# A hybrid attention and Fourier encoder on one core: stores at the end of the step, a second z buffer, one v load per block, and a new order of the side work

## The chip, the core and the metric

The kernel runs on one core of a Trainium2 chip. The core has five engines that run side by side and meet only through semaphores: TensorE (PE, matmuls; its weight loads are listed as PEld), VectorE (DVE), ScalarE (ACT), GpSimd (POOL) and SyncE (SP), which here issues nearly all transfers between the device memory and the core's own memory (SBUF). Every engine takes its instructions in the order in which the program has them; an instruction that waits holds all behind it on its engine. Matmul results lie in PSUM, which VectorE and ScalarE can read and GpSimd can't. The metric is the device time of one execution in microseconds.

## The reference

One encoder layer is applied to two sequences, a prompt of 256 tokens and a sample of 2048, each of width 1024. Cut to what matters:

```python
h = rms_norm(x, g_pre)
q, k, v, z_a, u_f, z_f = split(h @ w_in, 6)         # six times 512 columns
y_a = neighbourhood_attention(q, k, v, rpb)         # 8 heads of 64; tokens on a grid 64 wide;
                                                    # softmax over a window of 8 rows x 16 columns, with bias
y_f = real(fft2(u_f groups)) @ w_fourier + b_fourier
mixed = concat(rms_norm(y_a, g_na) * silu(z_a), rms_norm(y_f, g_f) * silu(z_f))
out = x + rms_norm(mixed @ w_out, g_post)
```

All is in float32; the kernel splits each factor of a product into a high and a low part and makes three matmuls of it.

## The kernel before

The first 600 us project x into q, k, v, z and u, store them in device memory, and do the Fourier half up to its result y_f, also stored. What the change touches is the stage behind it, the attention steps, which run from about 600 to 855 us; after that comes an output stage of 18 token tiles, which adds the attention half's share of `mixed @ w_out` to the Fourier half's share (stored as `oD`) and writes the output.

**The steps.** There are 36 groups of queries: four pairs of heads, nine groups each (one of the prompt, eight of the sample: four row ranges R, two column halves hc). The main loop has one step k per group. In step k TensorE computes the scores of group k (`scores`, L1229), transposes the softmax weights of group k-1 (`transp`, L1573, in two halves) and multiplies them with v (`pv`, L1589). VectorE adds the bias and takes the maximum (`bias_max`, L1251), ScalarE takes exponentials (`exps`, L1256), VectorE the reciprocal of the sum (L1260), GpSimd scales the weights (L1263); the transposes are copied out of PSUM by ScalarE and VectorE (L1575, L1577, tile `pt`); at the end of a step VectorE multiplies the product with the gate za into y (L1603). The halves of `transp` share PSUM banks `ptb`, so the second waits for the first's copies.

**The loads.** At a step's end `prep_v` loads v and za of group k+1, and `prep` the q of group k+4. v has three buffers. A group's v comes in two column blocks; each block is cut into chunks of up to 128 tokens, and where the last chunk is short it is loaded by a transfer of its own (L1197 and L1199).

**The stores.** The Fourier share's output rows (`oD`, L1530 and L1735) are issued when the tile is ready, and y (`yD`, L1612) when a tile of it is: in every second step, right behind L1603. As SyncE goes in order, what comes behind a store waits until its data are there.

**The side work.** TensorE's order is written out by hand: between the attention's matmuls it runs the Fourier share of the output product, plainly (`f_mm`) up to step 15. From step 16 on two token tiles at a time are done by a scheme that needs 7 products of blocks in place of 8, over four steps (`p_mm`; a pair of tiles begins at steps 16, 20, 24, 28 and 32). Its sums, high and low parts and evacuations on the other engines are placed by a table, `AT`: each entry names an operation, the step relative to the pair's first, one of ten slots in the step (called by `side`), and an engine. The names that matter here, with n for the step relative to the pair's first:

- M0, M1: y_f times z of the pair's two tiles (GpSimd, L1702). z has one buffer in `sm`: the second tile's z is loaded (L1473) only once M0 has read the first's.
- HD, LD: high and low part of the first tile; A1 to A4: sums of the tiles (L1712); H21, L21: high part (a cast, L1716) and low part (L1720) of a sum; H3, L3, H4, L4: further parts.
- X0 to X3, Z0, Z1, Z1b, Z2: evacuations of the products px and pz from PSUM into output rows `ofs` (L1729 adds, L1731 and L1733 only scale).

A second table, `TS`, places the preparation of the combined weights (`t_load`, `t_scale`, `t_sum`, `t_hi`, `t_lo`) in steps 9 to 16. The scores, px and pz share PSUM banks: four score tiles a step, three of the tag that pz has too.

Of the kernel before, what the change touches and what calls it, by code (L numbers as in the profile page):

```python
# [10 lines left out]
F32 = mybir.dt.float32  # L11
# [6 lines left out]
TP, TS = 256, 2048  # L18
# [12 lines left out]
K0 = (0, 4, 12, 20)  # L31
# [143 lines left out]
def build(tc, A, O):  # L175
    nc = tc.nc
# [8 lines left out]
    vD = [dr.tile([32, w, 512], F32, name="vD%d" % i) for i, w in enumerate(KW)]  # L185
# [585 lines left out]
    for b in range(16):  # L771
# [29 lines left out]
        if kind % 2:  # L801
            i, d = p, o
# [380 lines left out]
    def prep_v(g):  # L1183
        cs = slice(g["pr"] * 128, g["pr"] * 128 + 128)
        g["v"] = jl.tile([128, 7, 128], F32, tag="v", name="v", bufs=VB)
        g["ch"], j = [], 0
        for b, (c0, w) in enumerate(g["t"]):
            n = g["nr"] * w
            if g["R"] is None:
                src = vP[b]  # L1190
            else:
                src = vD[2 * g["hc"] + b][K0[g["R"]]:K0[g["R"]] + g["nr"]]
            src = src.rearrange("r c e -> (r c) e")
            m = -(-n // 128)
            z = min(-(-n // m) + 7 & ~7, 128)
            f = n // z
            nc.sync.dma_start(g["v"][:z, j:j + f], src[:z * f, cs].rearrange("(j p) e -> p j e", p=z))  # L1197
            if n % z:
                nc.sync.dma_start(g["v"][:n % z, j + f], src[z * f:, cs])  # L1199
            ch = [(z * x, min(z, n - z * x), j + x) for x in range(m)]  # L1200
            g["ch"].append(ch)
            j += len(ch)
        g["za"] = jl.tile([128, 256], F32, tag="za", name="za", bufs=VB)
        nc.sync.dma_start(g["za"], zD[1, cs, g["ts"]])
# [246 lines left out]
        later.append(second)  # L1451

    later = []

    def run_later():
        while later:
# [10 lines left out]
        if half and z:  # L1467
            z_load(d)

    def z_load(d):  # L1470
        ts = slice(d["t"] * 128, d["t"] * 128 + 128)
        d["z"] = sm.tile([128, 4, 128], F32, tag="yz", name="yz", bufs=1)
        nc.sync.dma_start(d["z"], zD[0, :, ts].rearrange("(c p) t -> p c t", p=128))  # L1473

    def ys_mul(d):
# [57 lines left out]

# [48 lines left out]
    def pv(g):  # L1582
# [26 lines left out]
            nc.scalar.activation(s4, p4, AF.Square)  # L1609
            nc.gpsimd.tensor_tensor(out=view(ysq[:, ts]), in0=view(ysq[:, ts]), in1=s4, op=ALU.add)  # L1610
        if R is None or hc:
            nc.sync.dma_start(yD[0, pr, :, ts], y)  # L1612

    WO = [[None, None] for c in range(4)]

# [41 lines left out]
    def t_lo(j, x, e):  # L1657
# [4 lines left out]
        else:  # L1662
# [4 lines left out]
    TS = ((9, 2, t_load, 0), (9, 6, t_load, 1), (10, 4, t_scale, 0), (11, 3, t_sum, 0, 0, V),  # L1667
          (11, 7, t_sum, 0, 1, V), (11, 8, t_scale, 1), (11, 8, t_sum, 0, 2, nc.gpsimd), (12, 2, t_sum, 1, 0, V),
          (12, 5, t_sum, 0, 3, V), (12, 7, t_sum, 1, 1, nc.gpsimd), (12, 5, t_hi, 0, 0, qt), (12, 6, t_hi, 0, 1, gt),
          (13, 1, t_lo, 0, 0, V), (13, 4, t_sum, 1, 2, V), (13, 6, t_hi, 1, 0, gt), (13, 8, t_sum, 1, 3, V),  # L1670
          (14, 2, t_lo, 1, 0, V), (14, 5, t_lo, 0, 1, V), (14, 7, t_hi, 1, 1, qt), (16, 6, t_lo, 1, 1, V))

    def B_(name):
        n, x = {"11": (0, 0), "21": (0, 2), "22": (1, 2)}.get(name, (None, None))
# [25 lines left out]
    def o_mul(P, e, x):  # L1700
        d = P["d"][x]
        e.tensor_tensor(out=d["raw"], in0=d["raw"], in1=d["z"], op=ALU.mult)  # L1702
        if x == 0:
            z_load(P["d"][1])

    def o_sum(P, e, x):
        if x == 0:
# [14 lines left out]
    def o_out(P, e, p, x, n, first, last):  # L1722
# [9 lines left out]
        else:  # L1732
            nc.scalar.activation(o[:, ns], i, AF.Copy, scale=s)  # L1733
        if last:
            nc.sync.dma_start(oD[t * 128:t * 128 + 128, :], o)  # L1735
# [9 lines left out]
    AT = (("A3", -1, 8, nc.gpsimd), ("H21", 0, 2, V), ("X2", 2, 3, V), ("M0", -3, 7, nc.gpsimd), ("L4", 2, 0, V),  # L1745
          ("X3", 3, 5, V), ("Z1", 1, 7, V), ("L3", 1, 2, V), ("A1", -1, 0, nc.gpsimd), ("X0", 0, 4, nc.scalar),
          ("A2", -1, 7, nc.gpsimd), ("M1", -2, 8, nc.gpsimd), ("Z0", 0, 8, V), ("X1", 1, 5, nc.scalar),
          ("L21", 0, 4, V), ("Z1b", 1, 7, V), ("H3", 0, 6, nc.scalar), ("HD", -2, 6, nc.scalar),
          ("H4", 1, 8, nc.scalar), ("LD", -2, 7, V), ("A4", 0, 7, nc.gpsimd), ("Z2", 2, 7, V))

    def side(k, slot):
        pr, i = divmod(k, 9)
# [60 lines left out]
    for k in range(2, len(G) + 1):  # L1813
# [222 lines left out]
```

## Time and profile before

| | |
|---|---|
| three runs, median (lowest to highest) | 966.48 us (963.81 to 970.37) |
| the profiled execution | 968.52 us |
| its span, first to last instruction | 966.7 us |
| mean granted clock of TensorE | 0.998 |
| busy TensorE, VectorE, ScalarE, GpSimd | 948.1, 738.4, 503.3, 453.9 us |
| transfers | 271.90 MB, mean 281 GB/s |

In the rows of the profile a line ends with the idle time of the engine before it and what released it (`[1.47 <-DMA v<-vD]`). A group of waits is "who waited, for whom: us in total, times, longest". `out<-in` are the program's names: `pt<-ptb` is the copy of the transposes. SPq stands for SyncE's queue; its rows are the moments of issue, and a long one is an issue that was held. Matmuls overlap: each is drawn longer than the distance to the next. Step k begins with its first matmul of L1229: step 16 at 708.82 us, step 22 at 753.06, step 24 at 769.30.

### The profile page before, as it was taken

What the parts mean: (1) busy time and instruction counts of PE and PEld (TensorE: products, weight loads), DVE (VectorE), ACT (ScalarE), POOL (GpSimd) and SP (SyncE); (2) the same over time, 40 slices, a digit from 0 to 9 for tenths busy, and PEclk for the clock granted to TensorE, in tenths of its full rate; (3) what the DMA queues carried; (4) which work ended last, traced back from release to release, by engine and by line L of the source; (5) the groups of instructions that cost most, each with busy time, mean ns of one, the idle gap of its engine ahead of it and who ended that gap; (6) DMA issues with size and microseconds to landing.
All of it is one profiled execution on the core that took longest, in us unless ns stands there. A gap on an engine that the chain in (4) does not pass through costs nothing. (4 is left out here: it accounts for less than half of the span.)

```text
span 966.7 us, 16758 instructions
## 1 busy us (share of the span) xinstructions
PE 948.1 (98%) x5595; PEld 785.2 (81%) x5595; DVE 738.4 (76%) x1347; ACT 503.3 (52%) x1083; POOL 453.9 (47%) x431
## 2 busy tenths in 40 slices
PE   9999999999999999999999999999998999999996
PEld 8889988888888888888888789787777777888875
DVE  6758987878976755797877378776987788759777
ACT  6736675433225432333344277777865666744443
POOL 4100003364842102755654065666897798625444
PEclk9999999999999999999999999999999999999999
DMA  9799697566749882599889987779875999989996
GB/s 358 290 379 339 242 355 252 196 213 258 302 153 381 299 340 101 211 366 339 304 300 341 365 278 269 230 221 303 261 239 179 286 280 278 295 300 330 290 309 217
DMA packets 140654, 271.90 MB, mean 281 GB/s; under 512 B 13242, under 2 KB 80528, under 8 KB 137304
## 3 DMA queue, kind: packets, MB, share of 16 engines
q1 hardware_dynamic: 140216, 270.41, 80.8%
q8 instruction: 45, 0.74, 0.3%
q10 hardware_dynamic: 288, 0.40, 0.1%
q14 instruction: 41, 0.34, 0.1%
q0 software_dynamic: 64, 0.02, 0.0%
HBM read 181.10 MB, written 96.81 MB: 287 GB/s over the span
## 5 line engine op out<-in xcount | busy, mean ns | idle before, releaser
L164 PE MATMUL mm<-xh,wa 128*128 128x512 f32 x448 | 174.6, 390 | 0.0
L166 PE MATMUL mm<-xh,wa 128*128 128x512 f32 x448 | 174.5, 389 | 0.0
L165 PE MATMUL mm<-xl,wa 128*128 128x512 f32 x448 | 174.5, 389 | 0.0
L545 POOL TENSOR_TENSOR ws<-wr 128x512 f32<-128x512 f32 x16 | 22.5, 1405 | 220.7 <-PE mm L166 125.4
L1263 POOL TENSOR_SCALAR w<-w,m 128x465 f32<-128x465 f32 (+9 forms) x136 | 91.0, 681 | 30.6 <-DVE m L1260 20.6
L164 PEld LDWEIGHTS mm<-xh,wa 128*128 128x128 f32 x448 | 84.1, 188 | 17.5
L165 PEld LDWEIGHTS mm<-xl,wa 128*128 128x128 f32 x448 | 84.1, 188 | 17.5
L166 PEld LDWEIGHTS mm<-xh,wa 128*128 128x128 f32 x448 | 84.1, 188 | 17.4
L1500 PE MATMUL po<-wk,yh 128*128 128x512 f32 x280 | 87.2, 393 | 0.3 <-ACT yh L1486 0.3
L560 DVE TENSOR_TENSOR wa<-wr,wa 128x512 fp32r<-128x512 f32 x60 | 70.7, 1186 | 20.3 <-ACT wa L559 20.0
L1256 ACT ACTIVATE w<-w,m 128x465 f32<-128x465 f32 (+9 forms) x136 | 78.4, 579 | 13.7 <-DVE m L1251 13.3
L1963 POOL TENSOR_TENSOR xt<-of,xt 128x512 f32<-128x512 f32 x34 | 43.2, 1291 | 54.5 <-issue 32.9
L1251 DVE CUSTOM_DVE_ANT_1 w<-s,tb 128x465 f32<-128x465 f32 (+8 forms) x124 | 61.3, 529 | 8.9 <-PE s L1229 7.4
L598 POOL TENSOR_TENSOR mt<-mt,rmask 128x880 f32<-128x880 f32 (+2 forms) x24 | 51.2, 2146 | 32.1 <-DVE mt L594 25.8
L165 PE MATMUL mm<-vl,xh 128*128 128x512 f32 x168 | 65.4, 390 | 0.0
L164 PE MATMUL mm<-vh,xh 128*128 128x512 f32 x168 | 65.4, 389 | 0.0
L166 PE MATMUL mm<-vh,xl 128*128 128x512 f32 x168 | 65.4, 389 | 0.0
L1589 PE MATMUL pv<-pt,v 120*64 120x128 f32 (+9 forms) x880 | 58.4, 278 | 5.5 <-DMA v<-vD 3.7
L1589 PEld LDWEIGHTS pv<-pt,v 120*64 120x64 f32 (+9 forms) x880 | 48.3, 136 | 19.1 <-issue 9.2
L891 DVE TENSOR_TENSOR f<-u,mm 128x512 f32<-128x512 f32 x64 | 43.5, 679 | 26.5 <-PE mm L166 20.1
L1573 PE MATMUL ptb<-ident,w 128*120 128x128 f32 (+8 forms) x422 | 59.8, 277 | 1.9 <-DVE pt L1577 1.1
L1500 PEld LDWEIGHTS po<-wk,yh 128*128 128x128 f32 x280 | 52.0, 188 | 11.7 <-ACT yh L1486 1.0
(333 smaller groups left out, 2457.7 us busy)
## 6 DMA issues: line engine op xcount, KB each, us to landing
wr<-wz SPq DMA_DIRECT2D x48, 512.0 KB
vl<-sD SPq DMA_DIRECT2D x20, 512.0 KB
xm<-xm SPq DMA_DIRECT2D x9, 1024.0 KB
oD<-ofs SPq DMA_DIRECT2D x18, 512.0 KB
of<-oD SPq DMA_DIRECT2D x18, 512.0 KB
xt<-xn SPq DMA_DIRECT2D x18, 512.0 KB
yo<-xt SPq DMA_DIRECT2D x35, 256.0 KB
yr<-yD SPq DMA_DIRECT2D x34, 256.0 KB
```

The lines of the kernel that those rows point to most:

```text
L164: nc.tensor.matmul(out, lh, rh, start=first, stop=False)
L165: nc.tensor.matmul(out, lh, rl, start=False, stop=False)
L166: nc.tensor.matmul(out, ll, rh, start=False, stop=last)
L560: nc.vector.tensor_tensor(out=o[:, 1], in0=src, in1=o[:, 0].bitcast(F32), op=ALU.subtract)
L598: nc.gpsimd.tensor_tensor(out=o, in0=i, in1=rmask[:, m0:m0 + n].unsqueeze(2).to_broadcast([128, n, 80]), op=ALU.add)
L891: nc.vector.tensor_tensor(out=dst(f, b), in0=src(uu[u]), in1=src(p), op=op)
L1251: nc.vector.tensor_tensor_reduce(out=rows(g["w"][b][:, h, :n], w), in0=rows(g["s"][2 * b + h][:, :nr * sw(w)], sw(w))[:, :, :w], in1=tv, s ...
L1256: nc.scalar.activation(w, w, AF.Exp, bias=m[:, h:h + 1], scale=-1.0, accum_out=m[:, 2 + h:3 + h])
L1263: nc.gpsimd.tensor_scalar(w, w, m[:, 4 + h:5 + h], 1.0, ALU.mult, ALU.mult)
L1500: nc.tensor.matmul(p, (d["l"] if x == 2 else d["h"])[:, c], w(n, int(x == 1), c), start=j == 0, stop=j == 11)
L1573: nc.tensor.transpose(ptb[h][:nk, j * 128:j * 128 + 128], g["w"][b][:, h, c0:c0 + nk], ident)
L1589: nc.tensor.matmul(p[hs, b], g["v"][:nk, v, hs], g["pt"][b][:nk, h, j * 128:j * 128 + 128], start=j == 0, stop=j == len(ch) - 1)
```

## The change

Four things change.

- Stores of y and of the output rows go onto a list (`put`) and are issued at the end of the step (`put_all`), behind the loads of v, za and q.
- The second tile's z of a pair gets a buffer of its own (pool `gz`) and is loaded three steps ahead together with its y, no longer after M0.
- Where the source has enough rows, a block of v is loaded in one transfer; the last chunk then brings some rows that are not used.
- The tables `TS` and `AT` have new places: among others A2 goes from GpSimd to VectorE (step n = -1, slot 5), X3 from VectorE to ScalarE, H21 moves from slot 2 to slot 1, LD from slot 7 to 6, X2 from slot 3 to 6, M1 and A1 to slot 1 of n = -1, A3 to slot 3 of n = 0.

```diff
@@ prep_v
-            if g["R"] is None:
-                src = vP[b]
-            else:
-                src = vD[2 * g["hc"] + b][K0[g["R"]]:K0[g["R"]] + g["nr"]]
-            src = src.rearrange("r c e -> (r c) e")
+            src = (vP[b] if g["R"] is None else vD[2 * g["hc"] + b][K0[g["R"]]:]).rearrange("r c e -> (r c) e")
             m = -(-n // 128)
             z = min(-(-n // m) + 7 & ~7, 128)
-            f = n // z
+            f = m if src.shape[0] >= m * z else n // z
             nc.sync.dma_start(g["v"][:z, j:j + f], src[:z * f, cs].rearrange("(j p) e -> p j e", p=z))
-            if n % z:
-                nc.sync.dma_start(g["v"][:n % z, j + f], src[z * f:, cs])
+            if f < m:
+                nc.sync.dma_start(g["v"][:n - z * f, j + f], src[z * f:n, cs])
...
+    puts = []
+
+    def put(dst, src):
+        puts.append((dst, src))
+
+    def put_all():
+        while puts:
+            nc.sync.dma_start(*puts.pop(0))
...
-    def z_load(d):
+    def z_load(d, pool=None):
         ts = slice(d["t"] * 128, d["t"] * 128 + 128)
-        d["z"] = sm.tile([128, 4, 128], F32, tag="yz", name="yz", bufs=1)
+        d["z"] = (pool or sm).tile([128, 4, 128], F32, tag="yz", name="yz", bufs=1)
...
@@ f_evac, o_out
-            nc.sync.dma_start(oD[t * 128:t * 128 + 128, :], o)
+            put(oD[t * 128:t * 128 + 128, :], o)
@@ pv
-            nc.sync.dma_start(yD[0, pr, :, ts], y)
+            put(yD[0, pr, :, ts], y)
...
@@ o_mul
-        if x == 0:
-            z_load(P["d"][1])
@@ AT, two of its lines
-          ("A2", -1, 7, nc.gpsimd), ("M1", -2, 8, nc.gpsimd), ("Z0", 0, 8, V), ("X1", 1, 5, nc.scalar),
+          ("HD", -2, 5, nc.scalar), ("M0", -3, 9, nc.gpsimd), ("A2", -1, 5, V), ("X3", 3, 7, nc.scalar),
...
@@ side
                 ys_load(P["d"][1], False)
+                z_load(P["d"][1], gz)
@@ main loop, end of step k
             gq = pt.enter_context(tc.tile_pool(name="gq", bufs=7, side="right"))
+            gz = pt.enter_context(tc.tile_pool(name="gz", bufs=1, side="right"))
         if k + 1 < len(G):
             prep_v(G[k + 1])
         if k + 4 < len(G):
             prep(G[k + 4])
+        put_all()
```

What stands on the engines is shown at three places. The first is SyncE between the ends of steps 17 and 18, from za and q of one group to the next v: vP holds the prompt's v, vD0 and vD1 the sample's, tb is the bias table, oD and yD are the stores. Before:

```order
L1197 DMA v_7415<-vP_68 80x2x128 x2
L1204 DMA za_7418<-zD_69 128x256
L1180 DMA ql_7421<-qD_62 128x2x128
L1154 DMA tb_7423<-tD15_81 128x2400
L1735 DMA oD_77<-ofs_7262 128x1024
L1612 DMA yD_78<-y_7410 128x512
L1197 DMA v_7519<-vD0_64 128x128
L1199 DMA v_7519<-vD0_64 125x128
L1197 DMA v_7519<-vD1_65 120x2x128
L1199 DMA v_7519<-vD1_65 101x128
L1204 DMA za_7524<-zD_69 128x256
```

And now:

```order
L1193 DMA v_7400<-vP_68 80x2x128 x2
L1200 DMA za_7403<-zD_69 128x256
L1180 DMA ql_7406<-qD_62 128x2x128
L1154 DMA tb_7408<-tD15_81 128x2400
L1193 DMA v_7501<-vD0_64 128x2x128
L1193 DMA v_7501<-vD1_65 120x3x128
L1200 DMA za_7504<-zD_69 128x256
L1180 DMA ql_7507<-qD_62 128x2x128
L1457 DMA oD_77<-ofs_7248 128x1024
L1457 DMA yD_78<-y_7394 128x512
```

The two stores stood between the table and v; they now stand behind v, za and q, and the four v loads of the group are two.

The second place is VectorE in step 16, around the cast H21 (L1716, now L1718): m is the reciprocal that the scaling of the weights waits for, L1661 (now L1665) a t_lo, pz the product whose bank the next scores need, y the product of pv and gate. Before:

```order
L1260 RECIPROCAL m_7215<-m_7215 128x2
L1716 CAST yh_7249<-ysum_7109 128x512
L1577 COPY pt_7253<-ptb_4833 120x384
L1720 TENSOR_TENSOR yl_7250<-ysum_7109,yh_7249 128x512
L1260 RECIPROCAL m_7216<-m_7216 128x2
L1661 TENSOR_TENSOR tl_7051<-wt_6501,th_7050 128x1024
L1729 SCALAR_TENSOR_TENSOR ofs_7262<-pz_7274,invf_92,ofs_7262 128x512
L1603 TENSOR_TENSOR y_7179<-pv_7285,za_7082 128x2x8x16
```

And now:

```order
L1718 CAST yh_7223<-ysum_7115 128x512
L1256 RECIPROCAL m_7199<-m_7199 128x2
L1581 COPY pt_7238<-ptb_4833 120x384
L1722 TENSOR_TENSOR yl_7224<-ysum_7115,yh_7223 128x512
L1256 RECIPROCAL m_7200<-m_7200 128x2
L1731 SCALAR_TENSOR_TENSOR ofs_7248<-pz_7256,invf_92,ofs_7248 128x512
L1665 TENSOR_TENSOR tl_7039<-wt_6505,th_7038 128x1024
L1607 TENSOR_TENSOR y_7162<-pv_7270,za_7065 128x2x8x16
```

The cast went ahead of the first reciprocal, and pz ahead of the t_lo.

The third place is VectorE at the end of step 18, where px, pz (X2, Z2) are evacuated and LD (yl from yr) is made; the same order comes in steps 22, 26 and 30. Before:

```order
L1260 RECIPROCAL m_7443<-m_7443 128x2
L1729 SCALAR_TENSOR_TENSOR ofs_7386<-px_7239,invf_92,ofs_7386 128x512
L1577 COPY pt_7473<-ptb_4833 96x384
L1260 RECIPROCAL m_7444<-m_7444 128x2
L1729 SCALAR_TENSOR_TENSOR ofs_7262<-pz_7490,invf_92,ofs_7262 128x512
L1720 TENSOR_TENSOR yl_7488<-yr_7219,yh_7487 128x512
L1603 TENSOR_TENSOR y_7410<-pv_7501,za_7309 128x2x8x16
```

And now:

```order
L1256 RECIPROCAL m_7428<-m_7428 128x2
L1581 COPY pt_7457<-ptb_4833 96x384
L1256 RECIPROCAL m_7429<-m_7429 128x2
L1731 SCALAR_TENSOR_TENSOR ofs_7373<-px_7226,invf_92,ofs_7373 128x512
L1722 TENSOR_TENSOR yl_7472<-yr_7203,yh_7471 128x512
L1731 SCALAR_TENSOR_TENSOR ofs_7248<-pz_7476,invf_92,ofs_7248 128x512
L1607 TENSOR_TENSOR y_7394<-pv_7484,za_7293 128x2x8x16
```

px left its place before the copy of pt, and LD went ahead of pz.

More of the change, by code (lines that the diff above doesn't have):

```diff
@@ L1665, in t_lo @@
             V.tensor_tensor(out=l[:, 1], in0=src[:, 1], in1=f_(h[:, 1]), op=ALU.subtract)
[L1667 to L1671, printed above, removed]
+    TS = ((9, 6, t_load, 0), (9, 8, t_load, 1), (10, 4, t_scale, 0), (11, 1, t_sum, 0, 0, V),
+          (11, 6, t_sum, 0, 1, V), (11, 7, t_scale, 1), (11, 8, t_sum, 0, 2, nc.gpsimd), (12, 6, t_sum, 1, 0, V),
+          (12, 5, t_sum, 0, 3, V), (12, 8, t_sum, 1, 1, nc.gpsimd), (12, 5, t_hi, 0, 0, qt), (12, 5, t_hi, 0, 1, gt),
+          (13, 1, t_lo, 0, 0, V), (13, 6, t_sum, 1, 2, V), (13, 6, t_hi, 1, 0, gt), (13, 8, t_sum, 1, 3, V),
+          (14, 3, t_lo, 1, 0, V), (14, 5, t_lo, 0, 1, V), (14, 8, t_hi, 1, 1, qt), (16, 7, t_lo, 1, 1, V))
     def B_(name):
@@ L1734, in o_out @@
         if last:
-            nc.sync.dma_start(oD[t * 128:t * 128 + 128, :], o)
+            put(oD[t * 128:t * 128 + 128, :], o)
     OPS = {"M0": (o_mul, 0), "M1": (o_mul, 1), "HD": (o_hi, "D"), "LD": (o_lo, "D"),
@@ L1744, in build @@
            "X3": (o_out, "X", 1, 0, True, True)}
-    AT = (("A3", -1, 8, nc.gpsimd), ("H21", 0, 2, V), ("X2", 2, 3, V), ("M0", -3, 7, nc.gpsimd), ("L4", 2, 0, V),
-          ("X3", 3, 5, V), ("Z1", 1, 7, V), ("L3", 1, 2, V), ("A1", -1, 0, nc.gpsimd), ("X0", 0, 4, nc.scalar),
-          ("A2", -1, 7, nc.gpsimd), ("M1", -2, 8, nc.gpsimd), ("Z0", 0, 8, V), ("X1", 1, 5, nc.scalar),
-          ("L21", 0, 4, V), ("Z1b", 1, 7, V), ("H3", 0, 6, nc.scalar), ("HD", -2, 6, nc.scalar),
-          ("H4", 1, 8, nc.scalar), ("LD", -2, 7, V), ("A4", 0, 7, nc.gpsimd), ("Z2", 2, 7, V))
+    AT = (("Z1", 1, 7, V), ("X2", 2, 6, V), ("Z0", 0, 7, V), ("H4", 1, 8, nc.scalar), ("X1", 1, 6, nc.scalar),
+          ("M1", -1, 1, nc.gpsimd), ("L4", 2, 0, V), ("L21", 0, 4, V), ("A4", 0, 5, nc.gpsimd),
+          ("X0", 0, 4, nc.scalar), ("A1", -1, 1, nc.gpsimd), ("LD", -2, 6, V), ("Z1b", 1, 7, V), ("Z2", 2, 7, V),
+          ("HD", -2, 5, nc.scalar), ("M0", -3, 9, nc.gpsimd), ("A2", -1, 5, V), ("X3", 3, 7, nc.scalar),
+          ("H3", 0, 7, nc.scalar), ("A3", 0, 3, nc.gpsimd), ("L3", 1, 2, V), ("H21", 0, 1, V))
     def side(k, slot):
```

## The prediction, made before the changed kernel ran

> **What bounds the kernel now.** First the page's head, then the busy time by stretch.
>
> ```profile
> span 966.7 us, 16758 instructions
> PE 948.1 (98%) x5595; PEld 785.2 (81%) x5595; DVE 738.4 (76%) x1347; ACT 503.3 (52%) x1083; POOL 453.9 (47%) x431
> ```
>
> TensorE is idle for 966.7 - 948.1 = 18.6 us in all. The change removes no matmul and leaves TensorE's order as it is, so it can win only idle time, and only in the attention steps.
>
> ```profile
> 650.00:700.00 50.00, 49.49 (x432) 39.26 (x430) 40.04 (x117) 38.24 (x109) 38.66 (x47) 1.00 0.87 273
> 700.00:750.00 50.00, 45.00 (x388) 35.77 (x388) 40.27 (x109) 32.21 (x95) 42.53 (x56) 1.00 0.70 214
> 750.00:800.00 50.00, 46.56 (x420) 36.96 (x419) 41.26 (x104) 31.68 (x90) 41.43 (x55) 1.00 0.94 287
> 800.00:855.00 55.00, 55.00 (x496) 44.43 (x495) 44.05 (x132) 36.87 (x111) 37.90 (x57) 1.00 0.89 278
> ```
>
> The columns are the stretch, its length, busy us of PE, PEld, DVE, ACT and POOL, the granted clock, the DMA share and GB/s. PE misses 0.5, 5.0, 3.4 and 0.0 us: nearly all the loss lies between 700 and 800 us (about steps 14 to 27). DMA there is idle first (0.70) and crowded after (0.94). The waits of PE between 600 and 855 us name the causes (us, times, longest):
>
> ```profile
> PE pv L1589 <- DMA v<-vD: 3.7, 3, 1.5
> PE pv L1589 <- DVE pt L1577: 1.9, 3, 1.1
> PE s L1229 <- DVE ofs L1729: 1.3, 2, 0.9
> PE ptb L1573 <- DVE pt L1577: 1.1, 2, 0.7
> PE ptb L1573 <- ACT pt L1575: 0.9, 2, 0.5
> ```
>
> These 12 waits make 8.9 us. Each costs a little more than it shows, as PE's own rows around the longest tell (start, length):
>
> ```profile
> 741.05 0.63 PE L1685 MATMUL pz<-wo,yh 128*128 128x512 f32 x2
> 741.51 0.39 PE L1685 MATMUL pz<-wo,yl 128*128 128x512 f32 x1
> 743.38 1.13 PE L1589 MATMUL pv<-pt,v 128*64 128x128 f32 x16 [1.47 <-DMA v<-vD]
> ```
>
> In full flow two matmuls start within 0.46 us (741.05 to 741.51), 0.23 each, yet one is drawn 0.39 long; so every wait hides 0.16 more. All twelve are then worth 8.9 + 12 x 0.16 = 10.8 us, the most the change can win if it touches nothing else: 1.1%.
>
> **The change part by part: SyncE's order.** SyncE issues almost every transfer, in order, and a transfer whose data are not ready holds all behind it. Its rows before the v waits, its wait for z between 700 and 800 us, and PE's first row of step 18:
>
> ```profile
> 713.37 0.45 SPq L1473 DMA_DIRECT2D yz<-zD  x1
> 719.52 0.33 SPq L1612 DMA_DIRECT2D yD<-y  x1
> 722.35 0.41 SPq L1466 DMA_DIRECT2D yr<-yD  x1
> 728.94 0.36 SPq L1473 DMA_DIRECT2D yz<-zD  x1
> 733.14 0.60 SPq L1197 DMA_DIRECT2D v<-vD  x1
> 736.75 5.53 SPq L1204 DMA_DIRECT2D za<-zD  x1
> SPq L1473 <- POOL yr L1702: 9.1, 2, 6.1
> 725.49 0.35 PE L1229 MATMUL s<-kh,qh 64*128 64x160 f32 x2
> ```
>
> SyncE stands still from 713.8 to 719.5 for the store of y, and from 722.8 to 728.9 because the second tile's z shares its one buffer with the first, which GpSimd multiplies late. Some 12 us late, the loads arrive in a lump: the v load for step 20's products goes out from 733.14, the next issue is held 5.53 us, and v misses its turn at 743.38. The change removes both causes: the store goes behind v, za and the q load; z gets its own buffer, last read two steps earlier. That v load then goes out once its buffer, read last in step 17, is free, at 725.49: up to 7.6 us more of room against 1.47 missing. The three v waits go: 1.47 and
>
> ```profile
> 745.63 0.44 PE L1589 MATMUL pv<-pt,v 101*64 101x128 f32 x4 [1.13 <-DMA v<-vD]
> 767.49 1.89 PE L1589 MATMUL pv<-pt,v 120*64 120x128 f32 x28 [1.06 <-DMA v<-vD]
> ```
>
> together 3.66 shown, -3.66 - 0.48 = -4.1 us. The same lateness held ScalarE, whose copy of px waits in line behind the q cast, and with it VectorE's addition and TensorE's next scores:
>
> ```profile
> 752.65 0.41 ACT L1208 CAST qh<-ql 128x256 fp32r<-128x256 f32 x1 [1.76 <-DMA ql<-qD]
> 754.49 0.43 PE L1229 MATMUL s<-kh,qh 64*128 64x360 f32 x2 [0.49 <-DVE ofs L1729]
> ```
>
> With q in time this goes too: -0.49 - 0.16 = -0.65. One v load instead of two saves SyncE an issue of about 0.4 us per step (722.35's length); the extra rows it fetches are a few KB. Neither is on a path. What the stores lose, some 2 us of delay, nobody waits for: y and oD are read again from step 32 on.
>
> **VectorE's order in steps 16 and 24.** The cast of the sum (H21) runs while GpSimd works through its list:
>
> ```profile
> L1716 DVE CAST yh<-ysum x5: 405/1269/4018, 712.2 to 828.4; 128x512 fp32r<-128x512 f32 x5
> 711.49 1.43 POOL L1141 TENSOR_TENSOR kl<-kl,kh 128x576 fp32r<-128x576 f32 x1
> 715.23 0.72 POOL L1209 TENSOR_TENSOR ql<-ql,qh 128x256 fp32r<-128x256 f32 x1
> L1712 POOL TENSOR_TENSOR ysum<-ysum,yr x5: 737/742/745, 710.8 to 825.2; 128x256 f32<-128x256 f32 x5
> 717.30 1.20 DVE L1661 TENSOR_TENSOR tl<-wt,th 128x1024 fp32r<-128x1024 f32 x1
> 716.76 0.87 PE L1589 MATMUL pv<-pt,v 120*64 120x128 f32 x10 [1.07 <-DVE pt L1577]
> 719.21 0.40 PE L1229 MATMUL s<-kh,qh 64*128 64x288 f32 x2 [0.85 <-DVE ofs L1729]
> 776.49 1.09 PE L1589 MATMUL pv<-pt,v 120*64 120x128 f32 x14 [0.29 <-DVE pt L1577]
> ```
>
> Of five casts the shortest took 0.405 us and the first, begun at 712.2, 4.018: it ended at 716.2, just when GpSimd's row of work ended (715.23 + 0.72 = 715.95). The copy of pt behind it came late (716.76, 1.07), and so did the evacuation of pz, also behind a t_lo of 1.20 us (719.21, 0.85). In the changed order the cast stands ahead of the reciprocal that GpSimd's next scaling needs, the sum A2 (0.742 us) has left GpSimd and A3 comes after that scaling. GpSimd then runs out of work after kl and ysq: 711.49 - 0.74 + 1.43 + 0.74 for ysq, of A2's size, is 712.9, and the cast ends near 713.4, 2.8 us sooner. The pz evacuation also passes t_lo. Both waits go, and 776.49, the same pattern in step 24: 1.07 + 0.85 + 0.29 = 2.21, with 3 x 0.16: -2.7 us.
>
> Here the Trainium skill (SBUF — State Buffer, "Who interferes with whom") says that VectorE and GpSimd share a port pair, which whoever starts first holds "for the whole instruction". By that a cast waits for one GpSimd instruction, 1.43 us at most; the trace differs, 4.02 us across a row of them. By the rule alone these 2.7 us would stay lost, the sum being -4.8; the measured row decides.
>
> **What moves onto the path.** A2 comes to VectorE, X3 leaves it for ScalarE, and the low part LD now stands ahead of pz's evacuation (Z2). No row shows A2 on VectorE; the nearest are
>
> ```profile
> L1720 DVE TENSOR_TENSOR yl<-yr,yh x10: 670/968/1809, 700.9 to 835.8; 128x512 fp32r<-128x512 f32 x10
> L1720 DVE TENSOR_TENSOR yl<-ysum,yh x10: 549/682/1497, 716.6 to 841.2; 128x512 fp32r<-128x512 f32 x5, 128x256 fp32r<-128x256 f32 x5
> L1731 DVE TENSOR_SCALAR ofs<-px,invf x5: 726/730/732, 736.1 to 852.0; 128x512 f32<-128x512 f32 x5
> L1733 ACT ACTIVATE ofs<-px,invf x10: 682/685/693, 713.2 to 837.5; 128x512 f32<-128x512 f32 x10
> ```
>
> A2 takes 0.55 to 1.50 us (the second row holds its shape), X3 gave back 0.73 in the same place: between -0.18 and +0.77 five times, hidden where VectorE waits for pv behind it; I take 0. ScalarE's 0.69 lies in idle time (it is busy 32 of 50 us above). LD ahead of Z2 delays the bank that the second half of the next scores needs by 0.67 to 1.81, at four pairs. Mostly the scores come later than that; I take a single hit near the lower end: +0.5, bounds 0 and 4 x 1.81 = 7.2.
>
> Five waits are left: in steps 14 and 15, where VectorE's order is the same, and in steps 22, 26 and 27. Half of two of those may go, as VectorE starts earlier: -0.5.
>
> **Sum:** -4.1 - 0.65 - 2.7 + 0.5 - 0.5 = -7.5 us. The profiled execution took 968.52 us (span 966.7 and 1.8 around it), so 961.0; the median of the runs, 966.48, lies 2.0 lower, which would make 959.0. I take 960.
>
> **The rivals.** *All waits go.* GpSimd gets 0.74 us lighter per pair and both engines start earlier, so the five left vanish and LD costs nothing: -10.8 us, 955.7 from the median, 957.7 from the profile. Against it: steps 14 and 15 see no change on VectorE.
>
> *Given back at the end.* In the output stage transfers are nearly full:
>
> ```profile
> 860.00:900.00 40.00, 40.00 (x192) 33.25 (x187) 34.87 (x71) 19.55 (x54) 16.04 (x13) 1.00 0.95 335
> 900.00:950.00 50.00, 49.69 (x215) 39.44 (x214) 36.61 (x87) 20.45 (x58) 20.93 (x17) 1.00 0.93 301
> ```
>
> If DMA at 0.95 sets that stage's end, up to all 7.5 us turn into waits there: 963 to 966.5. Against it, PE is busy for 40.00 of 40 us there, and its loads start earlier too.
>
> *The new order starves VectorE (slower).* A2 stands ahead of y in five steps and LD ahead of Z2 in four, each open to GpSimd. At worst 5 x 1.50 + 4 x 1.81 = 14.7 us, so 14.7 - 7.5 = +7.2 on the profile: about 974. It decides from 7.5 / 9 = 0.83 us lost per place. For it speaks the 1.81 row; against it, that the median there is 0.97, only 0.30 over the shortest. The skill's page Perfetto Trace Analysis ("Optimizing Scalar/DVE Operations") sides with this rival: moving work between GpSimd and VectorE "might not help", for they share a read port. No run yet shows A2 on VectorE.
>
> *The change does nothing:* v late for DMA's sake, not SyncE's. Then only the 2.7 and 0.65 could come: 964.
>
> **How the numbers follow.** Forecast 0.60, all waits go 0.13, given back or nothing 0.17, starved 0.10. The range runs from all waits gone, 955, to all given back, 966; outside is most of the starved case and a little of the others. A change of 1% (9.7 us) is about what a measurement of this kernel can tell from none: below 956.8 counts as faster. That needs nearly every wait gone: 0.20. Above 976.1 needs the starved case and more: 0.05. The rest, 0.75, lies within 1%, most of it on the faster side.
>
> **What would show it.** SyncE without the stands at 713 and 722; no PE wait on v; the first H21 under 1.5 us and the scores of step 17 without a wait; a DMA share near the 0.82 mean in both halves of 700 to 800. PE's idle sum over the steps near 3 us. Wrong would be new PE waits on pz after LD, on y after A2, or a longer output stage.

## The result, and the profile after

| | before | after |
|---|---|---|
| median (lowest to highest), 7 runs each on one chip | 966.83 us (963.81 to 970.37) | 958.86 us (957.58 to 962.04) |
| ratio, 95% interval | | 0.9917 [0.9896, 0.9938] |
| the profiled execution | 968.52 us | 958.19 us |

The change makes the kernel 0.83% faster, 8.0 us. The forecast was 960.0 us, 955 to 966, and within 1% with a chance of 0.75. The profiled execution of before lay 1.7 us above its median, that of after 0.7 below, so the two profiles differ by 10.3 us, more than the runs do.

In the changed file the lines have moved: the scores are L1225 (L1229), transp L1577 (L1573), pv L1593 (L1589), the copies of pt L1579 on ScalarE and L1581 on VectorE, all stores L1457, the cast H21 L1718 (L1716), A1 to A4 L1714 (L1712), the adding evacuation L1731 (L1729). First the head of after's page, with span and busy time of the engines.

```profile
span 956.4 us, 16730 instructions
PE 944.8 (99%) x5595; PEld 784.3 (82%) x5595; DVE 732.0 (77%) x1347; ACT 505.8 (53%) x1088; POOL 453.3 (47%) x426
```

TensorE was idle for 18.6 us and is now for 956.4 - 944.8 = 11.6. Next the waits of PE in the attention steps (600 to 845 us of after: us, times, longest).

```profile
PE ptb L1577 <- ACT pt L1579: 1.2, 2, 0.7
PE ptb L1577 <- POOL ysq L1614: 0.2, 1, 0.2
```

Twelve waits of 8.9 us have become three of 1.4 us. No wait on v is left, none on the scores' banks. The busy time by stretch says the same (length, PE, PEld, DVE, ACT, POOL, clock, DMA share, GB/s):

```profile
650.00:700.00 50.00, 50.00 (x448) 40.14 (x445) 39.17 (x119) 39.57 (x111) 40.31 (x48) 1.00 0.99 294
700.00:750.00 50.00, 48.80 (x427) 39.18 (x424) 40.84 (x120) 35.00 (x102) 45.65 (x60) 1.00 0.88 266
750.00:800.00 50.00, 49.77 (x453) 40.63 (x453) 39.74 (x121) 37.77 (x109) 45.01 (x61) 1.00 0.99 283
```

From 700 to 800 us TensorE now misses 1.2 and 0.2 us in place of 5.0 and 3.4. The length of the attention steps can be read from the groups of their first and last matmuls: the times of the first and last start stand behind the durations (min/median/max). In before:

```profile
L1229 PE MATMUL s<-kh,qh x140: 267/382/491, 591.1 to 848.1; 64*128 64x360 f32 x32, 64*128 64x480 f32 x32, 64*128 64x288 f32 x16, 64*128 64x384 f32 x16
L1589 PE MATMUL pv<-pt,v x880: 269/273/325, 604.8 to 860.3; 120*64 120x128 f32 x85, 105*64 105x128 f32 x19, 80*64 80x128 f32 x16, 96*64 96x128 f32 x12
```

and in after:

```profile
L1225 PE MATMUL s<-kh,qh x140: 267/381/490, 591.1 to 837.8; 64*128 64x360 f32 x32, 64*128 64x480 f32 x32, 64*128 64x288 f32 x16, 64*128 64x384 f32 x16
L1593 PE MATMUL pv<-pt,v x880: 270/272/324, 604.9 to 850.1; 120*64 120x128 f32 x84, 105*64 105x128 f32 x20, 80*64 80x128 f32 x16, 96*64 96x128 f32 x12
```

From the first score to the last product with v: 860.3 - 591.1 = 269.2 us before, 850.1 - 591.1 = 259.0 after. The rest up to the end is 966.7 - 860.3 = 106.4 and 956.4 - 850.1 = 106.3. So the whole difference of the two profiles, 10.2 us, lies in the attention steps, and the output stage gave nothing back. Its transfers are as full as they were: the prediction shows 0.95 and 0.93 for the 90 us from 860 us on; in after, the 90 us from 847 on, which begin some 3 us earlier in the work, have

```profile
847.00:887.00 40.00, 40.00 (x203) 33.16 (x202) 33.84 (x73) 19.56 (x54) 14.19 (x12) 1.00 0.95 328
887.00:937.00 50.00, 49.15 (x215) 39.87 (x214) 37.25 (x85) 20.82 (x61) 22.23 (x18) 1.00 0.92 298
```

SyncE's rows of after in the place that the prediction speaks of (start, length of the issue):

```profile
715.54 0.33 SPq L1457 DMA_DIRECT2D yD<-y  x1
717.62 0.36 SPq L1470 DMA_DIRECT2D yr<-yD  x1
718.04 0.78 SPq L1477 DMA_DIRECT2D yz<-zD  x1
718.91 0.95 SPq L1193 DMA_DIRECT2D v<-vP  x2
...
721.70 0.88 SPq L1193 DMA_DIRECT2D v<-vD  x2
722.90 0.68 SPq L1200 DMA_DIRECT2D za<-zD  x1
723.67 0.92 SPq L1180 DMA_DIRECT2D ql<-qD  x1
729.72 0.33 SPq L1457 DMA_DIRECT2D oD<-ofs  x1
```

The v load for step 20 goes out from 721.70; it was 733.14. That is just behind the first row of step 18 (721.59 us in after, 725.49 in before), as the prediction has it. SyncE still stands still for a store, from 724.6 to 729.7, but v, za and q are out by then. VectorE's casts and the sum A2 in their groups:

```profile
L1718 DVE CAST yh<-ysum x5: 421/533/762, 710.9 to 817.7; 128x512 fp32r<-128x512 f32 x5
L1714 DVE TENSOR_TENSOR ysum<-ysum,yr x5: 404/425/543, 706.0 to 812.6; 128x256 f32<-128x256 f32 x5
```

The longest of the five casts went from 4.018 to 0.762 us, and A2 takes 0.425 us (median) on VectorE, where GpSimd had needed 0.742.

### The profile page after: what moved, and what is told of

It reads as the page before. It is cut to its first block, busy times and chain, and to the rows that moved or that the text cites. A ratio compares the mean times of both kernels' runs of the same rounds, so it can differ in the third digit from the quotient of the medians.

```text
span 956.4 us, 16730 instructions
## 1 busy us (share of the span) xinstructions
PE 944.8 (99%) x5595; PEld 784.3 (82%) x5595; DVE 732.0 (77%) x1347; ACT 505.8 (53%) x1088; POOL 453.3 (47%) x426
## 2 busy tenths in 40 slices
DMA packets 140790, 272.17 MB, mean 285 GB/s; under 512 B 12854, under 2 KB 80664, under 8 KB 137440
## 4 chain that ended last, share of the span: by engine, by line
PE 89%; DMA 4%; DVE 2%; POOL 2%; ACT 1%; issue 1%; SPq 0%; DVEq 0%; POOLq 0%; ACTq 0%
PE mm L166 18%; PE mm L164 18%; PE mm L165 18%; PE po L1504 10%; PE ptb L1577 5%; PE pv L1593 5%; PE s L1225 4%; DMA yr<-yD 2%; PE px L1689 2%; PE pz L1689 2%; DMA yo<-xt 1%; PE py L164 1%; PE py L165 1%; PE py L166 1%; PE ptb L1043 1%
## 5 line engine op out<-in xcount | busy, mean ns | idle before, releaser
L560 DVE TENSOR_TENSOR wa<-wr,wa 128x512 fp32r<-128x512 f32 x60 | 75.4, 1264 | 21.9 <-ACT wa L559 21.6
L1577 PE MATMUL ptb<-ident,w 128*120 128x128 f32 (+8 forms) x422 | 59.0, 277 | 1.4 <-ACT pt L1579 1.2
L559 ACT CAST wa<-wr 128x512 fp32r<-128x512 f32 x60 | 36.5, 618 | 43.5 <-PE mm L166 20.4
L1577 PEld LDWEIGHTS ptb<-ident,w 128*120 128x120 f32 (+8 forms) x422 | 47.1, 140 | 14.5 <-issue 4.6
```

What stands on the lines that cost most here:

```text
L560: nc.vector.tensor_tensor(out=o[:, 1], in0=src, in1=o[:, 0].bitcast(F32), op=ALU.subtract)
L1577: nc.tensor.transpose(ptb[h][:nk, j * 128:j * 128 + 128], g["w"][b][:, h, c0:c0 + nk], ident)
```

## The experiments

Eleven kernels ran, and before once more. Each is compared with runs of before on the same chip, whose medians were 966.24, 966.34 and 967.08 us. "Steps" is the time from the first score to the last product with v, worked out as above, in the one profiled execution of each; "first cast" is H21 in step 16.

| kernel | median, us (runs) | ratio to before [95%] | steps, us | first cast, us |
|---|---|---|---|---|
| before, profile of the prediction | | | 269.2 | 4.02 |
| e12, before once more | 965.1 (1) | | 263.8 | 1.64 |
| e5, before with the cast ahead | 965.04 (12) | 0.9993 [0.9971, 1.0016] | 269.5 | 1.75 |
| e2, the two tables only | 967.89 (12) | 1.0022 [1.0005, 1.0039] | 265.8 | 0.72 |
| e3, stores at the end of the step only | 964.86 (12) | 0.9982 [0.9963, 1.0001] | 264.0 | 1.67 |
| e4, second z buffer only | 961.26 (12) | 0.9953 [0.9930, 0.9977] | 263.1 | 4.01 |
| e9, the first tile's z early | 961.90 (12) | 0.9949 [0.9930, 0.9969] | 261.7 | 4.03 |
| e1, all of SyncE's part, old tables | 959.28 (6) | 0.9928 [0.9903, 0.9952] | 259.2 | 1.66 |
| after | 958.86 (7) | 0.9917 [0.9896, 0.9938] | 259.0 | 0.76 |
| e6, after with the cast back | 959.98 (9) | 0.9944 [0.9923, 0.9966] | 259.1 | 0.68 |
| e7, after with two v loads | 959.97 (9) | 0.9945 [0.9926, 0.9964] | 259.0 | 0.74 |
| e8, after with two further moves | 959.13 (9) | 0.9937 [0.9916, 0.9958] | 259.6 | 0.80 |
| e10, after with A2 on GpSimd | 958.29 (6) | 0.9910 [0.9879, 0.9941] | 258.7 | 0.48 |
| e11, after with LD last | 958.78 (6) | 0.9917 [0.9885, 0.9949] | 258.8 | 0.75 |

The theory was that of the prediction: SyncE's order brings about 4.75 us, the tables about 2.7. The first rivals were that one of the two does it all.

### e1: SyncE's part alone

All of the diff but the tables `TS` and `AT`, which stay as they were before.

```diff
 # before, with
+    def put(dst, src): ...
+    def put_all(): ...
+    put(oD[...], o), put(yD[...], y)        # put_all() at the end of the step
+    z_load(P["d"][1], gz)                   # a buffer of its own
+    f = m if src.shape[0] >= m * z else n // z
```

> The kernel before with the stores at the step's end, the second z buffer and the single v load, and the old tables TS and AT. By the theory (late v and q come from SyncE standing still) the three PE waits on v and the one behind the q cast go: -4.1 - 0.65 = -4.8 us, ratio about 0.995; the cast H21 of step 16 still takes about 4 us and its two waits (1.07 and 0.85) stay. By the rival that v is late because the transfers themselves are slow, PE still waits on v for 2 us or more and the ratio is above 0.998. By the rival that the tables do all of it, nothing changes.

Measured: 959.28 us, 0.9928 [0.9903, 0.9952], or 0.72% x 966 = 7.0 us (4.6 to 9.4): nearly the whole gain. The waits of PE over the steps:

```profile
PE ptb L1577 <- ACT pt L1579: 0.9, 2, 0.5
PE s L1225 <- DVE ofs L1731: 0.8, 1, 0.8
PE ptb L1577 <- DVE pt L1581: 0.3, 1, 0.3
```

No wait on v is left, and none of VectorE's copy of pt ahead of pv (L1589 <- L1577 in the profile before, 1.9 us in three), although H21 stands behind the reciprocal as it did. What is left of the pair in step 16 is the wait for pz, 0.8.

### e2: the tables alone

Before with the new `TS` and `AT`, nothing else.

```diff
-          ("A2", -1, 7, nc.gpsimd), ("M1", -2, 8, nc.gpsimd), ("Z0", 0, 8, V), ("X1", 1, 5, nc.scalar),
+          ("HD", -2, 5, nc.scalar), ("M0", -3, 9, nc.gpsimd), ("A2", -1, 5, V), ("X3", 3, 7, nc.scalar),
 # and all other lines of TS and AT as in the change
```

> The kernel before with the new tables TS and AT alone; stores, z buffer and v loads as before. By the theory the waits behind H21 go (-2.7 us) and those on v stay (3.7 us shown): ratio about 0.997. By the rival that the new order starves VectorE it is above 1.0. By the rival that the tables do all of it, 0.992.

Measured: 967.89 us, 1.0022 [1.0005, 1.0039]: no gain, rather 2 us lost. Its waits of PE, the two largest groups:

```profile
PE pv L1589 <- DMA v<-vD: 3.3, 2, 1.8
PE s L1229 <- DVE ofs L1729: 2.0, 3, 1.0
```

The casts became short (0.72 in step 16), and the waits of steps 16 and 17 went. But the waits on v stayed, and the scores wait for evacuations in step 22 as before (0.46) and in two new places, at 807 and 815 us (0.50 and 1.00). So the 2.7 us put down to the tables don't come from them.

### e3 and e4: SyncE's part taken apart

e3 has the list of stores alone, e4 the z buffer alone.

```diff
 # e3
-            nc.sync.dma_start(yD[0, pr, :, ts], y)
+            put(yD[0, pr, :, ts], y)
 # the same for oD; put_all() at the end of the step
 # e4
-        if x == 0:
-            z_load(P["d"][1])
+                z_load(P["d"][1], gz)       # in side, with the tile's y
```

> The kernel before with only the stores put at the end of the step. SyncE is then still held until GpSimd has done M0, before the second tile's z (6.1 us at 722.8), so the v load for step 20 goes out only about 1 us earlier: I expect -1 us (ratio 0.999) with most of the PE waits on v left. The rival that the stores are what held v gives -4 us.

> The kernel before with only the second z buffer, loaded three steps ahead. The hold of 6.1 us before z goes; that before the store of y (5.7 us) stays, but the v load for step 20 goes out about 6 us earlier, which is more than the 1.5 us it missed: -4 us (ratio 0.996) with the PE waits on v gone. The rival that the stores are what held v leaves 3 us or more of waits and a ratio above 0.998.

Measured: e3 0.9982 [0.9963, 1.0001], 1.7 us or none; e4 0.9953 [0.9930, 0.9977], 4.5 us. The sum, 6.2, is near e1's 7.0. In e3 one wait on v is left, 1.7 us near 760, behind a z that GpSimd itself waited 5.4 us for at 761.6. In e4 none is left, although the stores stand ahead of v as before. Its rows on SyncE:

```profile
726.72 0.41 SPq L1154 DMA_DIRECT2D tb<-tD  x1
732.33 0.33 SPq L1733 DMA_DIRECT2D oD<-ofs  x1
733.48 0.32 SPq L1612 DMA_DIRECT2D yD<-y  x1
733.89 0.41 SPq L1197 DMA_DIRECT2D v<-vD  x1
...
735.50 1.03 SPq L1204 DMA_DIRECT2D za<-zD  x1
```

The v load of step 20 goes out at 733.89, no earlier than the 733.14 of before, and yet its product waits for nothing. What differs is what goes out just ahead of it. In before, behind the stand for z:

```profile
731.40 0.41 SPq L1154 DMA_DIRECT2D tb<-tD  x1
731.90 0.39 SPq L1735 DMA_DIRECT2D oD<-ofs  x1
732.73 0.32 SPq L1612 DMA_DIRECT2D yD<-y  x1
```

There the bias table tb (1200 KB), the largest load of the steps, went out 1.7 us ahead of v and the za behind v was held for 5.53 us; in e4 it went out 7.2 us ahead of v, and the za was held for 1.03. (The expectation had v go out 6 us earlier in e4; the store behind the table, which stood until 732.33, held it.)

The other traces agree. In e12, e5 and e2, where SyncE stands for z as in before, the table goes out 1.5 to 1.8 us ahead of v, za is held for 3.47 to 6.46 us, and the products of step 20 wait 1.2 to 2.3 us for v. In e9, with the buffer, the table is 7.1 us ahead, za is held for 0.85 and no product waits for v. So the lateness of the issue alone wasn't what made v late; it counted because table and v were issued in one lump, in which v takes longer. The stores need not be in the lump: in e3 none stands between table and v, za is held for 5.38 us all the same, and v is in time because it has 9.9 us to its product, where before it had 8.8. In after, too, the table goes out 0.8 us ahead of v, but v has 17 us. That the table's transfer is what slows v is read from these orders; no run took the table away.

The third wait of before, at 767 us, is another case. There the table goes out 2.8 to 4.7 us ahead of v in before, e12, e5 and e2, and 4.5 in e4; v has 6.1 to 7.4 us to its product in the first four and is late, and 8.7 us in e4 and is in time. In this place it is the lateness of the issue that makes the difference.

### e5 and e6: is it the place of the cast?

e5 moves H21 alone in before; e6 moves it back alone in after.

```diff
 # e5, in before's AT
-("H21", 0, 2, V)
+("H21", 0, 1, V)
 # e6, in after's AT
-("H21", 0, 1, V)
+("H21", 0, 2, V)
```

> The kernel before with one entry of AT changed: the cast H21 in slot 1, ahead of the reciprocal. By my theory of the cast (it is held as long as GpSimd has work in a row, and the withheld reciprocal ends that row) the first cast ends after GpSimd's sum A3 and ysq, about 1.5 us sooner, and the PE waits of steps 16 and 17 go (1.07 and 0.85 shown): ratio 0.998. By the rival that these waits hide in later ones, since the tables alone brought nothing, the cast is short and the ratio is 0.999 to 1.002.

> The changed kernel with the cast H21 back in slot 2, behind the reciprocal. If the place of the cast decides, its first one takes 1.5 us or more again and PE waits about 1 us in steps 16 and 17: ratio to before 0.993 instead of 0.992. If late loads had made the 4 us, it stays below 1.7 us, as with SyncE's part alone, and the ratio is that of the changed kernel.

Measured: e5 0.9993 [0.9971, 1.0016], with casts of 1.75 us in step 16 and 2.87 in step 24; e6 0.9944 [0.9923, 0.9966], with a cast of 0.68 in step 16 and of at most 0.43 in the others. In before's table the cast is as long ahead of the reciprocal (1.75) as in the executions e12, e1 and e3 behind it (1.64 to 1.67 in step 16); in the new table it is short behind it: its place isn't what decides. The reciprocal that is held back does end GpSimd's row of work, as the prediction says: in e5 GpSimd stands still 0.53 us for it behind ysq, and the cast ends in that gap. But this is neither needed for a shorter cast nor worth any time that shows.

### e7: is it the single v load?

```diff
-            f = m if src.shape[0] >= m * z else n // z
+            f = n // z
 # and the second load where n % z
```

> The changed kernel with v loaded in two transfers per block as before. By the theory an issue of 0.4 us more on SyncE, which no longer holds anything, costs nothing: ratio 0.991 to 0.993, no PE wait on v. The rival that the saved issues matter gives PE waits on v again and 0.994 or more.

Measured: 0.9945 [0.9926, 0.9964], with the same three waits of PE as after and none on v. The interval overlaps with after's, and e6, on the same chip and with the single load, took 959.98 us against 959.97: an effect of the single load on the time can't be seen. On SyncE there is one: behind the bias table at the end of step 17, za is held for 3.43 us in e7, and for 0.33 to 1.44 in the six kernels with the single load. Nothing waits for it.

### e8: the left-over waits

Two further moves in after, made to take away the waits that are left in steps 15 and 18: a t_lo a step later, and the scaling of the mask ahead of the split of q.

```diff
-(14, 5, t_lo, 0, 1, V)
+(15, 5, t_lo, 0, 1, V)
-            if k + 2 < len(G):
-                split_q(G[k + 2])
             if pr < 3 and i == 8:
                 mask_p(pr + 1)
+            if k + 2 < len(G):
+                split_q(G[k + 2])
```

> The changed kernel with two moves aimed at its two longest PE waits: the low part t_lo of the second weight from step 14 to 15, and GpSimd's mask of the bias table ahead of its q split. The waits of 0.48 and 0.70 us shown go, with 0.16 each: -1.5 us on the changed kernel, ratio to before 0.990. By the rival that a new wait takes their place the ratio stays at 0.992.

Measured: 0.9937 [0.9916, 0.9958]. The wait in step 15 went, the one in step 18 stayed (0.7), and three new ones came: on evacuations at 729 and 783 us (1.0 together) and for ScalarE at 659 (0.5). Here the half microseconds that were moved away came back at other places.

### e9 and e12: is it the late z?

In the profile before, GpSimd waited 1.69 us for the first tile's z at 696 us, and its work behind it began late. e9 loads that z a step earlier, into the second buffer; e12 is before, profiled once more.

```diff
 # e9, in before's side
+            if k - P["k"] == -5 and slot == 0:
+                z_load(P["d"][0], gz)
             if k - P["k"] == -4 and slot == 0:
-                ys_load(P["d"][0])
+                ys_load(P["d"][0], False)
```

> The kernel before with the first tile's z of a pair loaded a step earlier, into a buffer of its own; the second tile's z keeps its place in the program and so has the other buffer to itself. With the second z buffer alone GpSimd still waited 1.25 us for the first tile's z (M0 at 697 us) and the cast H21 of step 16 took 4.01 us. If that late z is what fills GpSimd's row and makes the cast long, GpSimd's wait at 695 to 698 us is gone, the cast takes 1.8 us or less, and the ratio is 0.993. If the cast is still near 4 us, the late z is not the cause.

> The kernel before once more, for a second profile. The first lost 8.9 us in 12 waits of PE in the attention steps, and its execution was 2 us above the median. If single executions differ in these waits, this one, if nearer the median, shows some 2 us less of them, mostly on v; if the waits are fixed by the program, the same 12 come again and the 2 us lie elsewhere.

Measured: e9 0.9949 [0.9930, 0.9969], as much as e4, whose second buffer it shares. But it did not do to the cast what it was made for: with z early, GpSimd waited as long for the y that goes with it. GpSimd's product M0 and VectorE's first cast in e9:

```profile
695.65 1.29 POOL L1702 TENSOR_TENSOR yr<-yr,yz 128x512 f32<-128x512 f32 x1 [1.80 <-DMA yr<-yD]
711.49 4.03 DVE L1716 CAST yh<-ysum 128x512 fp32r<-128x512 f32 x1
```

The same two in e4, and then in e12:

```profile
697.11 1.28 POOL L1702 TENSOR_TENSOR yr<-yr,yz 128x512 f32<-128x512 f32 x1 [1.25 <-DMA yz<-zD]
712.96 4.01 DVE L1714 CAST yh<-ysum 128x512 fp32r<-128x512 f32 x1
```

```profile
694.22 1.30 POOL L1702 TENSOR_TENSOR yr<-yr,yz 128x512 f32<-128x512 f32 x1 [0.49 <-DMA yz<-zD]
710.92 1.64 DVE L1716 CAST yh<-ysum 128x512 fp32r<-128x512 f32 x1
```

With the old table, the three executions in which GpSimd waited 1.25 to 1.80 us for that tile have casts of 4.01 to 4.03; the four with a wait of 0.49 or none (e12, e1, e3, e5) have 1.64 to 1.75. That is a relation over seven executions, not a test: the one kernel made to take the lateness away left it there.

e12 shows something else. Its waits of PE:

```profile
PE pv L1589 <- DMA v<-vD: 2.4, 2, 1.2
PE s L1229 <- DVE ofs L1729: 1.4, 2, 0.8
PE ptb L1573 <- DVE pt L1577: 0.9, 3, 0.4
PE ptb L1573 <- ACT pt L1575: 0.9, 2, 0.5
```

The same kernel, 5.6 us in place of 8.9, and steps of 263.8 in place of 269.2: two of the waits that the prediction priced (1.07 and 0.29, on VectorE's copy of pt) and one of the three on v aren't there. Over all profiles, the four executions that load as before (before, e12, e5, e2) have steps of 263.8 to 269.5 us, the seven with all of SyncE's part (but for e7's v loads) 258.7 to 259.6. The means differ by 267.1 - 259.1 = 8.0 us, as the medians do, and the scatter is gone: what the old order lost differed from one execution to the next.

Part of the scatter is TensorE's clock. In e5, TensorE stands idle for most of 741 to 743 us (the wait on v of 1.85), and from 745 to 748 its granted clock is 0.50 (the columns are those of the stretches above):

```profile
741.00:743.00 2.00, 0.28 (x6) 0.03 (x1) 0.00 (x0) 0.00 (x0) 0.00 (x0) 1.00 1.02 372
745.00:748.00 3.00, 3.00 (x12) 2.62 (x11) 2.26 (x9) 2.73 (x9) 2.56 (x6) 0.50 0.56 159
```

The same follows the idle time of 787 to 789 us in e5 and the wait of 1.73 us in e3. Taken over slices of 1 us, each time some 1.7 us of full clock are missing, which appear as no wait. Not every gap does this: behind the 1.81 us of e2 and the 1.47 of before the clock stays at 1.00, and these runs don't show what decides. The mean granted clock is 0.995 or lower in 23 of the 72 runs of before that the experiments were compared with; on each of the three chips these are longer in the mean than those with 0.997 or more, by 1.1 to 2.2 us. It is that low in none of the 52 runs with SyncE's part, e7's two v loads included.

### e10 and e11: A2 and LD

e10 gives A2 back to GpSimd, e11 puts LD behind Z2 again.

```diff
 # e10
-("A2", -1, 5, V)
+("A2", -1, 5, nc.gpsimd)
 # e11
-("LD", -2, 6, V), ("Z1b", 1, 7, V), ("Z2", 2, 7, V)
+("Z1b", 1, 7, V), ("Z2", 2, 7, V), ("LD", -2, 7, V)
```

> The changed kernel with the sum A2 back on GpSimd, in the same slot. If A2's leaving GpSimd is what made the cast short (0.76 us, against 1.66 us with SyncE's part alone), the cast of step 16 takes 1.4 us or more again. If A3's later slot did it, the cast stays under 1 us. Time: ratio to before 0.992 to 0.994 either way; by the rival that A2 on VectorE costs time, 0.990.

> The changed kernel with the low part LD behind the evacuation Z2 of pz, as before the change. By my prediction LD ahead of Z2 costs one hit of about 0.5 us; the changed kernel's profile shows no such wait in steps 19, 23, 27 and 31, so I now expect no difference: ratio to before 0.992 to 0.994, PE waits on ofs at most 0.5 us in sum.

Measured: e10 0.9910 [0.9879, 0.9941], e11 0.9917 [0.9885, 0.9949], neither to be told from after. In e10 the first cast stays short, with A2 (708.79) in GpSimd's row; GpSimd's rows and the cast:

```profile
708.79 0.73 POOL L1714 TENSOR_TENSOR ysum<-ysum,yr 128x256 f32<-128x256 f32 x1
709.48 1.44 POOL L1141 TENSOR_TENSOR kl<-kl,kh 128x576 fp32r<-128x576 f32 x1
710.87 0.93 POOL L1614 TENSOR_TENSOR ysq<-ysq,sqa 128x256 f32<-128x256 f32 x1
```

```profile
710.73 0.48 DVE L1718 CAST yh<-ysum 128x512 fp32r<-128x512 f32 x1
```

The next three casts take 0.75 to 0.91 us in e10 and 0.42 to 0.59 in after, so A2 on GpSimd costs them a little. But neither the place of the cast nor A2's leaving is what made the first one short. Of the three reasons of the prediction only A3's later place is left. It wasn't tried alone, and other moves of GpSimd's work (M0, M1, A1, A4) came with it, so which of them does it stays open.

## Why the prediction was right, and where not

**The bound.** Only idle time of TensorE could be won, at most 10.8 us in that execution: 10.2 came in the two profiles, 8.0 in the medians. This held, but what a wait hides was sized too small. With 1.4 us of waits left, 8.9 - 1.4 = 7.5 us of shown waits went, and the steps became 10.2 shorter. TensorE's busy time fell by 948.1 - 944.8 = 3.3 us, of which 1.8 are in the products with v and 0.8 in the transposes, whose matmuls are drawn longer around a wait: the 20 of step 20 took 1.13 + 0.44 us around their two waits and 1.32 in after. The 0.16 per wait, taken from a matmul of 512 columns, gives 9 x 0.16 = 1.4 us for the nine waits less, about half of the 10.2 - 7.5 = 2.7 us that the shown waits leave over.

**SyncE's order: right, but under-sized.** The three waits on v went (-4.1), and so did the wait of step 22 (-0.65). The whole part brings 7.0 us (4.6 to 9.4), not 4.75; the forecast of 4.75 is just inside the interval. The earlier issue of v came as argued, but two steps were too simple. The argument took the stores and z together as what holds v: the z buffer alone brings 4.5 us, the stores 1.7 or none. And it had only the earlier issue, "up to 7.6 us more of room", while e4 gets v in time with an issue as late as before, once table and v aren't issued in one lump. The sum also has no term for the clock that falls behind some of the waits.

**The cast H21: wrong in cause.** The term of -2.7 us was given to the tables; alone they bring +0.2%, in the interval 0.5 to 3.8 us slower. Of its three waits, those on the copy of pt (1.07 and 0.29) are not in e12 and not in e1: they came with the casts of 4.02 and 2.84 us of that execution. The first went along with a late tile on GpSimd, which comes from SyncE; that the one makes the other is not shown. In e4 and e9, where the cast takes 4 us and no wait on v is left, a wait of 1.1 for the copy of pt still stands. Only the wait for pz (0.85; 0.8 in e1, about as much in e12, none in after) belongs to the tables, and they pay it back: the wait in step 18,

```profile
725.39 0.94 PE L1577 MATMUL ptb<-ident,w 128*96 128x128 f32 x6 [0.70 <-ACT pt L1579]
```

is in e2 and in after but not in e1. With SyncE's part the tables are worth 959.28 - 958.86 = 0.4 us by the medians and 1.1 by the ratios, which these runs can't tell from nothing. That the forecast of 960 came so near is in part luck: SyncE's part was taken too small and the tables' too large by nearly the same amount.

The prediction set this against the Trainium skill (SBUF — State Buffer, "Who interferes with whom"), which says that whoever issues first has the shared port pair "for the whole instruction"; it read from this that a cast waits for one GpSimd instruction. Casts of 4.02, 4.01 and 4.03 us in three executions, across rows whose longest GpSimd instruction takes 1.44, disagree with that reading. The sum by the rule was -4.8; what the prediction drew from the row instead, that the new order wins the difference, was not borne out either.

**LD ahead of Z2: +0.5 taken, 0 found.** After has no wait of the scores in its list, and e11 takes the order back to no effect. **A2 and X3: 0 taken, 0 found.** A2 takes 0.425 us, less than the 0.55 to 1.50 of the prediction's row, and e10 shows no effect of its engine on the time. Here the Trainium skill (Perfetto Trace Analysis, "Optimizing Scalar/DVE Operations"), which says that such a move "might not help", agrees with the runs: it neither helped nor harmed. **The left-over waits: half of two taken.** Of the five, 2.5 us, two are left with 0.7, and the new one of step 18 has 0.70.

**The profile against the median.** The prediction saw that its profiled execution lay above the median and took 960 between 959.0 and 961.0. It did not ask whether the waits that it priced are the same in each execution; e12 says no.

**The rivals.** All waits go: nearly, in number, but steps 15 and 18 still wait, and 958.9 is not 955.7. Given back at the end: no, 106.4 against 106.3 us behind the last product with v. VectorE starved: no, its busy time fell by 6.4 us. (The 974 of this case is the median plus 7.2; on the profile, as it says there, it would be 975.7.) The change does nothing: no for SyncE's part; it is true of the tables.

**What was to show it.** The stands of SyncE at 713 and 722, the waits on v, the long first cast and the wait of step 17 are gone, as said. PE's idle time in the steps was put near 3 us; it is 1.4. The DMA share was put near 0.82 in both halves of 700 to 800 us; it is 0.88 and 0.99. The bytes are nearly the same (272.17 MB against 271.90), but the steps that load them take 10 us less, and a share of 0.99 made no wait.

## What to carry to other kernels

Before a wait gets a price and a cause, look whether a second execution of the same kernel has it, and whether two waits on different engines go back to one late load; else the same gain is booked to the wrong edit. In a queue that issues in order, give a reload a buffer of its own before moving the stores about: a load that waits for a reader holds all loads behind it, and then they go out in a lump; here the buffer was worth 4.5 us, and moving the stores 1.7 or nothing. Try each part of a change alone and also undo it in the whole: here the tables looked like a third of the gain in the trace and were worth nothing either way.

## What the runs showed of the hardware

- A cast on VectorE that takes 0.41 us by itself took 4.01 to 4.03 us in three executions, until a row of six GpSimd instructions had ended, the first of which was running when it began; begun at nearly the same place of the program, it took 1.64 to 1.75 in four others, and 0.48 in e10, where it ended while a GpSimd instruction was running, which took 0.93 us against 0.73 for the same instruction in e6. What lets a cast in between two GpSimd instructions at one time and not at another, these runs don't show.
- The issue of za on SyncE, which takes 0.3 to 0.5 us where nothing holds it, was held for 3.4 to 6.5 us in six executions in which four v loads followed the bias table within 1.8 us, and for 0.85 and 1.03 in the two (e9, e4) in which the table had gone out 7 us earlier.
- Behind waits that show 1.73 us (e3), 1.85 and 2.0 us (e5), the granted clock of TensorE fell to 0.50 for 3 to 4 us; behind waits of 1.81 us (e2) and 1.47 us (before) it did not.
- The same sum of 128x256 elements took 0.742 us on GpSimd and 0.425 on VectorE.
